# Splitting the weights of the backward pass: single steps through the end of the attention pass, none on GpSimd, a third in the next pass

## The chip, the cores and the metric

The kernel runs on one core of one Trainium2 chip. The metric is the device time of one execution in microseconds (us). A core has TensorE for matrix products (PE in the profile, its weight loads PEld), VectorE (DVE), ScalarE (ACT), GpSimd (POOL) and the DMA queues, of which SyncE (SP) issues most. Each engine takes its instructions in a fixed order; an instruction that waits holds everything behind it on its engine. About 0.2% is what a measurement of this kernel can tell from no change.

## The reference

One layer of a bidirectional encoder over 4096 rows of 1024 values, float32, in two groups of heads behind one normalised input projection.

```python
hn = rms_norm(x, norm_w)
proj = hn @ w_in                       # all groups' columns at once
qk_a = silu(conv5(qk_a))               # group A: centred depthwise conv over 5 rows
h = sigmoid(o_a) * (mlstm(q, k, v, i_f, f_f) + flip(mlstm(flip(q), flip(k), flip(v), i_b, f_b)))
y_a = head_rms_norm(h) * silu(z_a)     # 4 heads x 128, chunks of 128 rows
y_b = windowed_gqa(q_b, k_b, v_b, sink, rel_bias) * silu(z_b)   # |i-j| <= 128, 8 heads / 2 kv heads x 64
out = rms_norm(x + concat(y_a, y_b) @ w_out, final_norm_w)
```

The gate logits of group A go through `log_sigmoid`, running sums and running maxima along the rows before the two scans can use them.

## The kernel before

The kernel makes float32-like products from a cheaper format: each operand is split into a rounded part and the remainder, and three products (high x low, low x high, high x high) are added in one PSUM bank. A weight is split in two steps: ACT writes the rounded part scaled by the row's norm weight `nw`, DVE writes the remainder (`scalar_tensor_tensor`).

The work goes in passes. The **attention pass** (`pass1`) takes the rows in 16 blocks of 256 (`b`), with 32 chunks of 128 (`n`). It projects queries (`qproj`, tile `qp`, evicted by DVE at L538), keys (`kproj`, `kp`) and values and gates (`vproj`, `vp`, gates added by POOL at L509), and does the windowed attention of group B in **slots**: slot `sl` is one chunk and one of two kv heads. A slot is a list of up to ten pieces: scores of the slot after next (`att_a`, tile `sp`, evicted at L362 with row maxima; L369 makes the shift `st`), transposes of its probabilities (`att_t`, `tp`, split into `pt` by ACT L389 and DVE L390), and products with the values of the slot before (`att_o`, tile `op`, L401). `op` has one PSUM bank; ACT (L413) and DVE (L414) bring it into `ab`, which has one buffer too, and SP sends `ab` to DRAM (L416). The next slot's first `op` waits for L414.

TensorE's order is written by hand. `interleave(fill, pieces)` spreads the projections' matmuls (`fill`, with costs) evenly between the pieces: piece i comes when i/len(pieces) of the filler's cost is done. The other engines' orders are made from it by a scheduler, which follows the order of the program but lets ready work go ahead. `behind(c, ins)` holds an instruction back until `ins` stands.

The last three blocks run as one list, `pieces`, with **hooks** inserted at positions: the gate computations `gate1` to `gate3`, and `w2_load(j, c0)`, which loads and splits the weights that the next pass needs: values (j = 0), keys (j = 1) and queries (j = 2) of group A, each as 8 steps `k` of 128 rows x 512 columns. A step has a staging tile `w2s` of the tag `xf` (two buffers); every fourth step is scaled and subtracted on GpSimd (L554, L556) with a cast on ACT (L555), the others go through ACT (L558) and DVE (L559). The filler ends with the first value products of group A (`v2_units`, tile `v2p`).

The **backward pass** (`pass2`) goes through eight blocks of 512 rows from the last to the first: values (`v2p`, L829), keys (`qkproj` with m = 4 to 7) and queries (m = 0 to 3; tile `up`, L856; DVE does the convolution at L874 and L877), transposes of keys (`ktp`, tile `kt`, four buffers), weighting of the values (`weigh`: `wvr`, `wvh`, `wvl`) and state products (`kvp`, tile `kv`, L158 to L160; state `C`). `place(fill, pieces)` puts `ktp` and `kvp` at given shares of the filler. Block 7, the first that is done, uses the rows still on the chip; the loads `xb` of block 6 are issued during it.

## Time and profile before

| | before |
|---|---|
| median of 3 runs | 2211.6 us |
| lowest, highest | 2209.2, 2212.46 us |
| the profiled execution's own time | 2211.38 us |
| its span, first to last instruction | 2209.7 us |
| granted TensorE clock, mean | 0.994 |
| PE busy | 2163.6 us, 98% |
| DVE, ACT, POOL busy | 1409.6, 1086.3, 608.1 us |
| chain that ended last | PE 77%, DMA 8%, issue 5%, DVE 5%, ACT 2%, POOL 2% |

A line of groups names the source line, the engine, the operation, the tiles written and read, the shape and the count; then busy time and the mean of one in ns, and the idle time before them with what ended it. In the list by time the first numbers are start and length; the brackets hold the idle time before and its releaser. The attention pass lasts up to about 609 us; the weights in question are loaded and split from 444 to 599 us of the span.

### The profile page before, as it was taken

Reading aid. Unit: us, or ns where it says so; the run is one execution under the profiler, and the core shown is the slowest. Engines: PE = TensorE matmul, PEld = TensorE weight load, DVE = VectorE, ACT = ScalarE, POOL = GpSimd, SP = SyncE. Lnnn points to the kernel's source line nnn. Section 1 sums busy time; section 2 is a strip of 40 time slices with the busy share of each in tenths; the row PEclk is TensorE's granted clock in tenths of the full one; section 3 lists DMA queues with packets and bytes.
Section 4 is the critical chain, followed back from the end, with each engine's and each line's share of the span. In section 5 each row is a group of like instructions: output and inputs, shape, how many; then the busy total and the mean of one; then the engine's idle time right before and its main releaser. Section 6 shows DMA issues by size and latency. Waiting matters only on the chain.

```text
span 2209.7 us, 35186 instructions
## 1 busy us (share of the span) xinstructions
PE 2163.6 (98%) x12226; PEld 1878.6 (85%) x12226; DVE 1409.6 (64%) x3090; ACT 1086.3 (49%) x2711; POOL 608.1 (28%) x1059
## 2 busy tenths in 40 slices
PE   7999999999999999999999999999999999999998
PEld 6899999998797888888887888888888888888886
DVE  4677777777874575566568645455554443867776
ACT  5788888886743343344345444444443321433333
POOL 2565665662121211121112111112111111112222
PEclk9999999999999999999999999999999999999999
DMA  7663555432224442454166976877685899666765
GB/s 234 187 162 110 171 141 127 157 108 77 87 78 130 159 146 67 142 163 142 58 212 198 324 229 217 250 228 219 222 259 185 298 353 294 186 180 189 199 187 147
DMA packets 249126, 398.98 MB, mean 181 GB/s; under 512 B 21971, under 2 KB 128467, under 8 KB 248948
## 3 DMA queue, kind: packets, MB, share of 16 engines
q1 hardware_dynamic: 220628, 303.57, 45.3%
q0 software_dynamic: 28176, 92.96, 13.0%
q8 instruction: 96, 1.57, 0.3%
q14 instruction: 82, 0.67, 0.1%
q10 hardware_dynamic: 144, 0.20, 0.0%
HBM read 275.99 MB, written 120.67 MB: 180 GB/s over the span
## 4 chain that ended last, share of the span: by engine, by line
PE 77%; DMA 8%; issue 5%; DVE 5%; ACT 2%; POOL 2%; SPq 0%; POOLq 0%; DVEq 0%; ACTq 0%
PE up L856 15%; PE zp L1153 7%; PE qp L524 7%; PE op L1153 7%; PE v2p L829 7%; DMA xr<-x 5%; PE op L401 4%; PE tp L387 3%; PE sp L359 3%; PE zbp L158 3%; PE zbp L160 3%; PE zbp L159 3%; PE num L1106 3%; PE num L1105 2%; PE o L1320 2%
## 5 line engine op out<-in xcount | busy, mean ns | idle before, releaser
L856 PE MATMUL up<-xb,w 128*128 128x512 f32 x1344 | 338.4, 396 | 0.0
L1320 PE MATMUL o<-wo,yo 128*128 128x512 f32 (+1 forms) x1356 | 312.2, 392 | 0.0
L1320 PEld LDWEIGHTS o<-wo,yo 128*128 128x128 f32 x1356 | 253.2, 188 | 59.1
L856 PEld LDWEIGHTS up<-xb,w 128*128 128x128 f32 x1344 | 243.7, 188 | 47.2
L874 DVE SCALAR_TENSOR_TENSOR qk<-U,cw,qk 128x512 f32<-128x512 f32 x256 | 190.1, 755 | 94.2 <-ACT qk L872 89.4
L524 PE MATMUL qp<-xT,wqb 128*128 128x256 f32 x1536 | 246.3, 291 | 0.0
L524 PEld LDWEIGHTS qp<-xT,wqb 128*128 128x128 f32 x1536 | 218.0, 193 | 9.9 <-issue 1.7
L1153 PE MATMUL op<-w,xs 128*128 128x512 f32 x720 | 201.7, 407 | 0.0
L1153 PE MATMUL zp<-w,xs 128*128 128x512 f32 x720 | 187.9, 401 | 1.5 <-DVE z L1163 1.5
L829 PE MATMUL v2p<-w,xb 128*128 128x512 f32 x672 | 157.9, 395 | 1.9 <-DMA xb<-xT_d 1.9
L1153 PEld LDWEIGHTS zp<-w,xs 128*128 128x128 f32 x720 | 130.9, 189 | 28.4 <-DVE z L1163 2.0
L829 PEld LDWEIGHTS v2p<-w,xb 128*128 128x128 f32 x672 | 126.0, 188 | 32.5 <-DMA xb<-xT_d 3.2
L362 DVE CUSTOM_DVE_ANT_0 s<-sp,G 128x320 f32<-128x320 f32 (+1 forms) x256 | 122.8, 480 | 42.6 <-PE sp L359 39.4
L390 DVE TENSOR_TENSOR pt<-tp,pt 128x512 fp32r<-128x512 f32 x188 | 129.3, 688 | 26.6 <-ACT pt L389 25.1
L371 ACT ACTIVATE s<-s,st 128x320 f32<-128x320 f32 (+1 forms) x256 | 139.8, 549 | 12.0 <-DVE st L369 11.5
L1153 PEld LDWEIGHTS op<-w,xs 128*128 128x128 f32 x720 | 126.7, 189 | 20.9
L389 ACT CAST pt<-tp 128x512 fp32r<-128x512 f32 x188 | 110.0, 586 | 61.2 <-PE tp L387 58.4
L1120 ACT ACTIVATE hs<-num,r 128x128 f32<-128x128 f32 x128 | 47.1, 368 | 182.4 <-DVE r L1117 155.4
L401 PE MATMUL op<-pt,v 128*128 128x512 f32 x376 | 121.6, 405 | 11.7 <-DVE ab L414 11.7
L359 PE MATMUL sp<-kk,q 128*128 128x320 f32 (+2 forms) x512 | 118.9, 313 | 0.0
L387 PE MATMUL tp<-ident,s 128*128 128x128 f32 x752 | 113.9, 274 | 1.5 <-DVE pt L390 1.2
L1143 POOL DMA_DIRECT2D y_d<-ya x32 | 19.4, 607 | 325.4 <-ACT hs L1120 182.5
(273 smaller groups left out, 4530.1 us busy)
## 6 DMA issues: line engine op xcount, KB each, us to landing
xc<-xT_d SPq DMA_DIRECT2D x64, 512.0 KB, 8.0
xs<-xT_d SPq DMA_DIRECT2D x120, 256.0 KB, 6.5
xT_d<-xT POOLq DMA_DIRECT2D x104, 256.0 KB, 5.2
xb<-xT_d SPq DMA_DIRECT2D x48, 514.0 KB, 10.1
E<-m_d SPq DMA_DIRECT2D x64, 256.0 KB, 4.8
W<-w_d SPq DMA_DIRECT2D x64, 256.0 KB, 5.8
y<-y_d SPq DMA_DIRECT2D x32, 512.0 KB, 3.4
out<-xr POOLq DMA_DIRECT2D x31, 512.0 KB, 4.3
```

What stands on the lines that cost most here:

```text
L359: nc.tensor.matmul(sp[:, lo:hi], qt, kk[:, kv, z, col - 128 + lo:col - 128 + hi], start=(z == 0), stop=(z == 1))
L362: nc.vector.tensor_tensor_reduce(out=s[:, lo:hi], in0=sp[:, lo:hi], in1=bias[0][:, kv * 2 + m, lo - 64 * half:hi - 64 * half], op0=ALU.add ...
L371: nc.scalar.activation(ps[g][:, kept(g)], ps[g][:, kept(g)], AF.Exp, bias=ng[:, g:g + 1], accum_out=rs[:, g:g + 1])
L387: nc.tensor.transpose(tp[:, g * 128:(g + 1) * 128], ps[g][:, j * 128:(j + 1) * 128], c.ident)
L390: nc.vector.tensor_sub(pt[:, 1, :], tp, f32(pt[:, 0, :]))
L401: nc.tensor.matmul(op, vt, pt[:, z, :], start=(i == 0 and z == 0), stop=(i == len(js) - 1 and z == 1))
L524: nc.tensor.matmul(qp, wq[k // 2][:, k % 2, w, m * 128:m * 128 + 128], x[k], start=(k == 0 and j == 0), stop=(k == KT - 1 and j == 2))
L829: nc.tensor.matmul(vp, a, wv[k // 2][:, k % 2, m, :], start=(k == 0 and j == 0), stop=(k == KT - 1 and j == 2))
L856: nc.tensor.matmul(up[:, 0:hi - lo], w[k // 2][:, k % 2, a, cs], x, start=(k == 0 and j == 0), stop=(k == KT - 1 and j == 2))
L874: nc.vector.scalar_tensor_tensor(acc, U[:, t:t + 512], cw[:, cm, t:t + 1], acc, ALU.mult, ALU.add)
L1153: nc.tensor.matmul(P[nm], XS[n](a, k), w[:, m, :], start=(k == 0 and j == 0), stop=(k == KT - 1 and j == 2))
L1320: nc.tensor.matmul(p, a[:, z, k, :], w[k // 2][:, k % 2, m, lo:hi], start=k == 0 and z == 1, stop=k == 3 and z == 0 and m == 0)
```

## The change

`w2_load` is replaced by `w2_piece(j, k)`, one step of 128 rows, for values and keys alone. Values' steps 0 to 3 go into the slots of the last regular block (b = 12), steps 4 to 7 at positions 42 to 50 of the final list, keys' steps 0 to 7 at positions 68 to 96, four apart. All steps are split by ACT and DVE (`w2_split`); the load is held behind the last `at_d` transfer and the split behind the last small exponential of ACT. `gate1` is cut in three parts at positions 54, 58 and 62 instead of one at 80. The queries' weights (j = 2) are loaded at the start of the backward pass into the four `kt` buffers, two steps at once, and split behind the key projections m = 5 and m = 6 of block 7; the first `kvp` of that block comes at 44/96 of the filler instead of 34/96.

```diff
-        def w2_load(j, c0):
-            out = []
-            for k in range(KT):
...
-                st = wk.tile([128, 512], F32, tag="xf", bufs=2, name=f"w2s{j}{k}")
-                nc.sync.dma_start(st, A["w_in"][k * 128:k * 128 + 128, c0:c0 + 512])
-                s = c.nw[:, k:k + 1]
-                if k % 4 == 0:
-                    nc.gpsimd.tensor_tensor(out=st, in0=st, in1=s.broadcast_to([128, 512]), op=ALU.mult)
-                    nc.scalar.copy(w[:, k % 2, 0, :], st)
-                    nc.gpsimd.tensor_tensor(out=w[:, k % 2, 1, :], in0=st, in1=f32(w[:, k % 2, 0, :]), op=ALU.subtract)
-                    continue
-                nc.scalar.activation(w[:, k % 2, 0, :], st, AF.Copy, scale=s)
-                nc.vector.scalar_tensor_tensor(w[:, k % 2, 1, :], st, s, f32(w[:, k % 2, 0, :]),
-                                               ALU.mult, ALU.subtract)
+        def w2_piece(j, k):
...
+            st = wk.tile([128, 512], F32, tag="xf", bufs=2, name=f"w2s{j}{k}")
+            with behind(c, LAST["at"]):
+                nc.sync.dma_start(st, A["w_in"][k * 128:k * 128 + 128, 512 * j:512 * j + 512])
+            with behind(c, LAST["act"]):
+                w2_split(c, w, st, k)
...
+            if b == NB - 4:
+                for i in range(4):
+                    A2.insert(3 + 5 * i, lambda i=i: w2_piece(0, i))
...
-        hooks = [(40, lambda: w2_load(0, 0)), (80, lambda: gate1(c, wk)), (100, lambda: gate2(c, wk)),
-                 (104, lambda: w2_load(1, 512)), (113, lambda: gate3(c, wk)), (113, lambda: w2_load(2, 1024))]
+        hooks = [(p, lambda k=k: w2_piece(0, k)) for k, p in zip(range(4, 8), (42, 44, 48, 50))]
+        hooks += [(54 + 4 * i, lambda i=i: gate1(c, wk, i)) for i in range(3)]
+        hooks += [(68 + 4 * k, lambda k=k: w2_piece(1, k)) for k in range(8)]
+        hooks += [(100, lambda: gate2(c, wk)), (113, lambda: gate3(c, wk))]
...
+def w2_split(c, w, st, k):
+    s = c.nw[:, k:k + 1]
+    c.nc.scalar.activation(w[:, k % 2, 0, :], st, AF.Copy, scale=s)
+    c.nc.vector.scalar_tensor_tensor(w[:, k % 2, 1, :], st, s, f32(w[:, k % 2, 0, :]), ALU.mult, ALU.subtract)
...
-        wv, wk_, wq = c.w2
+        wv, wk_ = c.w2
+        wq = [wtile(c, [128, 2, 2, 512], f"w2_2{j}") for j in range(4)]
+
+        wqs = []
+        for j in range(4):
+            wqs.append(wk.tile([128, 2, 512], F32, tag="kt", bufs=4, name=f"w2s2{j}"))
+            nc.sync.dma_start(wqs[j], win_src(c, 2 * j, 2, 1024, 512))
+
+        def w2q(js):
+            with behind(c, c.ucopy):
+                for j in js:
+                    for i in range(2):
+                        w2_split(c, wq[j], wqs[j][:, i], 2 * j + i)
...
+                if b == 7 and m in (5, 6):
+                    w2q((0, 1) if m == 5 else (2, 3))
...
-            at += [((34 + 62 * (4 * (n3 - n) + hh) / 16) / 96, lambda n=n, hh=hh: kvp(n, hh))
+            k0 = 44 if b == 7 else 34
+            at += [((k0 + (96 - k0) * (4 * (n3 - n) + hh) / 16) / 96, lambda n=n, hh=hh: kvp(n, hh))
                    for n in range(n3, n3 - 4, -1) for hh in range(NH)]
```

Three places on DVE show what this does to the order. In the names, `w2_JK` is the weight j = J, of the pair of steps that begins with K, and `w2sJK` the staging tile of step K; the digits behind `pt`, `tp`, `sp`, `op` are the slot, behind `ab` and `vg` the chunk; the last number only counts.

DVE at the end of block 12, up to the eviction of slot 50 into `ab25`, before:

```order
L499 TENSOR_TENSOR vg28_6976<-vp28_6937,vg28_6976 128x144
L362 ISA s1_5_161,st53_6932<-sp53_3_7017,G_91 128x320
L362 ISA st53_6932 128x1
L559 SCALAR_TENSOR_TENSOR w2_00_7491<-w2s01_7497,nw_88,w2_00_7491 128x512
L369 SCALAR_TENSOR_TENSOR st53_6932<-st53_6932,nsink_228 128x4
L390 TENSOR_TENSOR pt51_1_6998<-tp51_1_6993,pt51_1_6998 128x512
L362 ISA s0_0_150,st54_7056<-sp54_0_7057,G_91 128x320
L362 ISA st54_7056 128x1
L414 TENSOR_TENSOR ab25_7007<-op50_6942,ab25_7007 64x2x4x64
```

and with the change:

```order
L499 TENSOR_TENSOR vg28_6990<-vp28_6946,vg28_6990 128x144
L636 SCALAR_TENSOR_TENSOR w2_02_6951<-w2s02_6952,nw_88,w2_02_6951 128x512
L636 SCALAR_TENSOR_TENSOR w2_02_6951<-w2s03_7000,nw_88,w2_02_6951 128x512
L362 ISA s1_5_161,st53_6941<-sp53_3_7037,G_91 128x320
L362 ISA st53_6941 128x1
L390 TENSOR_TENSOR pt51_1_7018<-tp51_1_7013,pt51_1_7018 128x512
L503 TENSOR_TENSOR v28_6993<-vg28_6990,v28_6993 128x2x64
L369 SCALAR_TENSOR_TENSOR st53_6941<-st53_6941,nsink_228 128x4
L362 ISA s0_0_150,st54_7074<-sp54_0_7075,G_91 128x320
L362 ISA st54_7074 128x1
L376 RECIPROCAL R_92<-st52_6827 128x4
L414 TENSOR_TENSOR ab25_7032<-op50_6958,ab25_7032 64x2x4x64
```

Two splits, of steps 2 and 3, stand where one of step 1 stood; steps 0 and 1 now stand as another pair ahead of `ab24`.

DVE ahead of the eviction of slot 56 into `ab28`, in the final list, before:

```order
L390 TENSOR_TENSOR pt57_0_7674<-tp57_0_7669,pt57_0_7674 128x512
L362 ISA s1_4_160,st59_7646<-sp59_2_7692,G_91 128x320
L538 SCALAR_TENSOR_TENSOR q15_1_7678<-qp15_1_7607,q15_1_7678 64x4x64 x2
L559 SCALAR_TENSOR_TENSOR w2_12_8177<-w2s12_8178,nw_88,w2_12_8177 128x512
L559 SCALAR_TENSOR_TENSOR w2_12_8177<-w2s13_8182,nw_88,w2_12_8177 128x512
L390 TENSOR_TENSOR pt57_1_7704<-tp57_1_7699,pt57_1_7704 128x512
L362 ISA s1_5_161,st59_7646<-sp59_3_7720,G_91 128x320
L414 TENSOR_TENSOR ab28_7713<-op56_7654,ab28_7713 64x2x4x64
```

and with the change:

```order
L636 SCALAR_TENSOR_TENSOR w2_06_7589<-w2s06_7590,nw_88,w2_06_7589 128x512
L636 SCALAR_TENSOR_TENSOR w2_06_7589<-w2s07_7631,nw_88,w2_06_7589 128x512
L390 TENSOR_TENSOR pt57_0_7665<-tp57_0_7660,pt57_0_7665 128x512
L362 ISA s1_4_160,st59_7638<-sp59_2_7697,G_91 128x320
L660 TENSOR_SCALAR g0_7678<-g0_7678 128x256
L538 SCALAR_TENSOR_TENSOR q15_1_7689<-qp15_1_7627,q15_1_7689 64x4x64 x2
L661 RECIPROCAL g0_7678<-g0_7678 128x256
L390 TENSOR_TENSOR pt57_1_7709<-tp57_1_7704,pt57_1_7709 128x512
L414 TENSOR_TENSOR ab28_7718<-op56_7647,ab28_7718 64x2x4x64
```

The two splits moved up by a few instructions, and the gate chain's first steps (`g0`, with the reciprocal) stand here, which came some three slots later before.

DVE at the start of the backward pass, block 7, after the fourth instruction of the first key convolution, before:

```order
L877 SCALAR_TENSOR_TENSOR qk7_4_8390<-th7_4_8396,qk7_4_8390 128x512
L874 SCALAR_TENSOR_TENSOR qk7_5_8455<-U7_5_8400,cw_7932,qk7_5_8455 128x512 x4
L877 SCALAR_TENSOR_TENSOR qk7_5_8455<-th7_5_8461,qk7_5_8455 128x512
L744 COPY cl_8132<-mp_8530 128x4
L745 TENSOR_SCALAR cl_8132<-cl_8132 128x2
```

and with the change:

```order
L900 SCALAR_TENSOR_TENSOR qk7_4_8360<-th7_4_8366,qk7_4_8360 128x512
L897 SCALAR_TENSOR_TENSOR qk7_5_8425<-U7_5_8370,cw_7672,qk7_5_8425 128x512
L636 SCALAR_TENSOR_TENSOR w2_20_8290<-w2s20_8294,nw_88,w2_20_8290 128x512
L897 SCALAR_TENSOR_TENSOR qk7_5_8425<-U7_5_8370,cw_7672,qk7_5_8425 128x512
L636 SCALAR_TENSOR_TENSOR w2_20_8290<-w2s20_8294,nw_88,w2_20_8290 128x512
L636 SCALAR_TENSOR_TENSOR w2_21_8291<-w2s21_8296,nw_88,w2_21_8291 128x512
L897 SCALAR_TENSOR_TENSOR qk7_5_8425<-U7_5_8370,cw_7672,qk7_5_8425 128x512
L636 SCALAR_TENSOR_TENSOR w2_21_8291<-w2s21_8296,nw_88,w2_21_8291 128x512
L897 SCALAR_TENSOR_TENSOR qk7_5_8425<-U7_5_8370,cw_7672,qk7_5_8425 128x512
```

Four of the eight splits of the queries' weights stand between the steps of one convolution; the other four stand between those of the next.

More of the change, by code (lines that the diff above doesn't have):

```diff
@@ L542, in qproj @@
             return [(lambda m=m, k=k, j=j: unit(m, k, j)) for m in range(4) for k in range(KT) for j in range(3)]
[L544 to L561 removed]
+        def w2_piece(j, k):
+            if k == 0:
+                c.w2.append([])
+            if k % 2 == 0:
+                c.w2[j].append(wtile(c, [128, 2, 2, 512], f"w2_{j}{k}"))
+            w = c.w2[j][k // 2]
+            st = wk.tile([128, 512], F32, tag="xf", bufs=2, name=f"w2s{j}{k}")
[3 more added lines that the diff above has]
+                w2_split(c, w, st, k)
         def v2_units(ns):
@@ L662, in gate1 @@
     nc.vector.tensor_scalar(e, f, 0.0, None, ALU.min)
-    nc.vector.scalar_tensor_tensor(c.GF.rearrange("p a h n -> p (a h n)"), p, -2.0, e, ALU.mult, ALU.add)
+    nc.vector.scalar_tensor_tensor(f, p, -2.0, e, ALU.mult, ALU.add)
     tri = c.tri = wk.tile([128, 2, 128], F32, tag="vg", bufs=2, name="tri")
```

45 lines of the change are left out of this document (24 added, 21 removed).

## The prediction

> **What bounds the kernel now.** The page first, for who is busy; then TensorE's own list of waits, for what holds it; then the granted clock by stretch; then the other engines' instructions in order of time around the longest wait.
>
> ```profile
> span 2209.7 us, 35186 instructions
> PE 2163.6 (98%) x12226; PEld 1878.6 (85%) x12226; DVE 1409.6 (64%) x3090; ACT 1086.3 (49%) x2711; POOL 608.1 (28%) x1059
> PE op L401 <- DVE ab L414: 11.7, 7, 3.5
> ```
>
> TensorE is busy 98% of the span, and its largest wait is `op`, the probabilities times values, on `ab`, the eviction of the one PSUM bank that `op` has. The list of TensorE's instructions with their idle time puts it (start, length, then in brackets the idle before and its releaser):
>
> ```profile
> 502.25 1.22 PE L401 MATMUL op<-pt,v 128*128 128x512 f32 x2 [3.51 <-DVE ab L414]
> 513.71 0.73 PE L401 MATMUL op<-pt,v 128*128 128x512 f32 x2 [0.65 <-DVE ab L414]
> 558.26 0.73 PE L401 MATMUL op<-pt,v 128*128 128x512 f32 x2 [1.59 <-DVE ab L414]
> 568.37 0.73 PE L401 MATMUL op<-pt,v 128*128 128x512 f32 x2 [1.76 <-DVE ab L414]
> 601.63 0.73 PE L401 MATMUL op<-pt,v 128*128 128x512 f32 x2 [1.07 <-DVE ab L414]
> 646.93 0.39 PE L159 MATMUL kv<-wvl,kt 128*128 128x258 f32 x1 [1.64 <-DVE wvl L920]
> 677.18 3.21 PE L829 MATMUL v2p<-w,xb 128*128 128x512 f32 x12 [1.47 <-DMA xb<-xT_d]
> 680.80 9.53 PE L829 MATMUL v2p<-w,xb 128*128 128x512 f32 x40 [0.41 <-DMA xb<-xT_d]
> ```
>
> So the change's own stretch, 440 to 680 us, holds 8.58 us of `op` waits over half a microsecond (five of them), 1.64 us for `wvl` and 1.88 us for `xb`. Idle time is not the whole loss. The clock falls behind two of these waits (windows: length, five engines' busy time with counts, clock, DMA share, GB/s):
>
> ```profile
> 502.00:504.00 2.00, 1.75 (x6) 1.55 (x7) 1.21 (x4) 1.73 (x6) 0.71 (x5) 0.50 0.28 96
> 504.00:506.00 2.00, 2.00 (x11) 2.00 (x11) 1.10 (x4) 0.00 (x0) 0.60 (x1) 0.50 0.37 131
> 506.00:508.00 2.00, 2.00 (x11) 1.86 (x10) 1.05 (x4) 0.58 (x1) 0.00 (x0) 0.61 0.43 104
> 568.00:570.00 2.00, 1.63 (x5) 1.35 (x6) 1.97 (x5) 2.00 (x9) 0.00 (x0) 0.75 0.70 223
> 570.00:572.00 2.00, 2.00 (x9) 1.70 (x9) 0.79 (x4) 0.06 (x1) 1.20 (x2) 0.50 0.51 147
> 572.00:574.00 2.00, 2.00 (x10) 1.68 (x10) 0.69 (x1) 1.72 (x3) 0.54 (x1) 0.90 0.10 35
> ```
>
> Busy time times the missing clock is lost: 1.75 x 0.50 + 2.00 x 0.50 + 2.00 x 0.39 = 2.65 us behind the first, 1.63 x 0.25 + 2.00 x 0.50 + 2.00 x 0.10 = 1.61 us behind the second, 4.26 us together. All that the change can win on TensorE is then about 8.6 + 4.3 + 1.6 + 1.9 = 16.4 us, 0.7% of the span.
>
> **What makes `ab` late.** DVE and GpSimd in order of time before the 3.51 us:
>
> ```profile
> 497.18 1.84 DVE L559 SCALAR_TENSOR_TENSOR w<-w2s,nw,w 128x512 fp32r<-128x512 f32 x1
> 498.95 1.65 DVE L369 SCALAR_TENSOR_TENSOR st<-st,nsink 128x4 f32<-128x4 f32 x1
> 501.53 0.67 DVE L414 TENSOR_TENSOR ab<-op,ab 64x512 f32<-64x512 f32 x1
> 513.69 0.16 DVE L369 SCALAR_TENSOR_TENSOR st<-st,nsink 128x4 f32<-128x4 f32 x1
> 497.17 1.30 POOL L556 TENSOR_TENSOR w<-w2s,w 128x512 fp32r<-128x512 f32 x1
> 498.42 1.11 POOL L509 TENSOR_TENSOR G<-vg,gb 128x4 f32<-128x4 f32 x4
> 499.49 1.08 POOL L265 TENSOR_TENSOR xT<-xraw,xT 128x512 fp32r<-128x512 f32 x1
> L559 DVE SCALAR_TENSOR_TENSOR w<-w2s,nw,w x18: 737/751/1844, 497.2 to 599.5; 128x512 fp32r<-128x512 f32 x18
> ```
>
> One split took 1.84 us where the median of 18 is 0.75, and the small `st` behind it 1.65 us where another took 0.16: 1.09 + 1.49 = 2.58 us of stretch, while GpSimd ran L556, L509 and L265 without a gap. Both stretched instructions read two operands from SBUF; the `ab` behind them reads one from PSUM and took 0.67, as `ab` does elsewhere. The Trainium skill, GPSIMD Engine Reference, section Key points, says that GpSimd shares its SBUF interfaces with VectorE and contends with instructions that have two SBUF inputs; the rows agree, and the rule speaks against this change too, for L509 and L265 stay while the number of splits beside them grows.
>
> **The change part by part.** The matmuls are the same. Removed from GpSimd are six multiplications and six subtractions; DVE and ACT take them over:
>
> ```profile
> L554 POOL TENSOR_TENSOR w2s<-w2s,nw x6: 1030/1040/1042, 446.9 to 581.9; 128x512 f32<-128x512 f32 x6
> L556 POOL TENSOR_TENSOR w<-w2s,w x6: 1278/1297/1516, 497.2 to 593.4; 128x512 fp32r<-128x512 f32 x6
> L558 ACT ACTIVATE w<-w2s,nw x18: 706/723/731, 496.4 to 598.5; 128x512 fp32r<-128x512 f32 x18
> ```
>
> GpSimd loses 6 x (1.04 + 1.30) = 14.0 us. DVE goes from 18 to 24 splits: +6 x 0.75 = 4.5 us. But by place: 4 now fall before 500 us (one before), 12 between 500 and 600 us (17 before), 8 into the next pass (none). Per place:
>
> First pair (k = 0 and 1, ahead of `ab24`). Nothing stood there. Two casts on ACT, 2 x 0.72 us, and two splits on DVE, 2 x 0.75 us, now stand ahead of the `pt` and `ab` of their slot, and behind that `ab` waits the first `op` of the next slot. The nearest row for a split ahead of an `ab` is the 0.65 us at 513.71. I take +0.5; bounds 0 (DVE's idle time takes the 1.5 us) and 1.5 (none of it does).
>
> Second pair (k = 2 and 3, ahead of `ab25`), the 3.51 us place. Before: one split, 2.58 us of stretch. Now a second split, +0.75, and L556 gone from GpSimd, while L509 and L265 remain and a cast of keys (L466) moves in between. Without any stretch the wait would be 3.51 - 2.58 + 0.75 = 1.7 us; with as much as before 4.3 us. I take 3.2, nearer the upper end, since what remains on GpSimd, 1.11 + 1.08 us, again begins when the `vg` ahead of the pair is done. So -0.3.
>
> Clock behind it: a wait of 3.2 us is nearest to the 3.51 that lost 2.65, so 0 change; bounds -2.65 and 0. By the Trainium skill, TensorE: Matmul & The Clock Gate, Part 1, the clock is halved only after an idle window of about 3.4 us; the row at 568.37, half clock behind 1.76 us, says that less is enough here, so I do not lean on it.
>
> The waits of 0.65, 1.59 and 1.76. Two splits stood directly ahead of the second of these `ab`, one ahead of each other. Now a split comes with every fourth piece, and as each piece gets the same share of the filler (132 pieces instead of 121, 17 of them hooks instead of 6), a slot that holds splits gets a tenth more TensorE time to hide them and one without gets a tenth less. I take all three waits as gone: -4.0 us; bounds -4.0 and 0. Each load follows an `at_d` on SP's queue, so none stands ahead of the transfer that `ab`'s single buffer needs; 20 issues instead of 24 cost nothing there. What comes instead is the gate chain, moved forward to where queries are still projected:
>
> ```profile
> L538 DVE SCALAR_TENSOR_TENSOR q<-qp,q 64x256 fp32r<-64x256 f32 x30 | 12.7, 422 | 1.7 <-ACT q L534 1.2
> L655 DVE RECIPROCAL g<-g 128x256 f32<-128x256 f32 x1 | 1.7, 1747 | 0.0
> 576.28 0.68 DVE L414 TENSOR_TENSOR ab<-op,ab 64x512 f32<-64x512 f32 x1 [0.18 <-ACT ab L413]
> 585.63 0.69 DVE L414 TENSOR_TENSOR ab<-op,ab 64x512 f32<-64x512 f32 x1
> ```
>
> Before, the reciprocal and its neighbours with two splits filled 9.35 us from one `ab` to the next without a wait. Now two stretches follow each other that share the chain and hold four evictions of queries each, 4 x 0.42 = 1.7 us, the first with two splits, the second without. I take 0.8 us; bounds 0 (as before) and 2.0 (both 1 us over). A clock drop behind it, 1.6 us, I weigh at a fifth: 0.3. The 1.07 at 601.63 stands where the attention runs out and three evictions follow closely; without the two splits ahead of it I take 1.0, since it also hangs on ACT.
>
> Next pass. Eight casts and splits, 8 x 0.75 = 6.0 us of DVE, go in between the convolutions. DVE is idle there (rows of DVE):
>
> ```profile
> 609.52 17.34 PE L856 MATMUL up<-xT,w 128*128 128x258 f32 x144
> 622.43 3.18 DVE L874 SCALAR_TENSOR_TENSOR qk<-U,cw,qk 128x512 f32<-128x512 f32 x4 [1.16 <-ACT qk L872]
> 635.77 1.54 DVE L874 SCALAR_TENSOR_TENSOR qk<-U,cw,qk 128x512 f32<-128x512 f32 x2 [2.12 <-ACT qk L872]
> ```
>
> A product of 48 matmuls takes 17.34 / 3 = 5.8 us, so the fifth, the first to need these weights, begins behind 609.5 + 4 x 5.8 = 632.7 us, and its last weights are wanted 2 us later. From 622.43 DVE has 3.18 us of convolution and 6.0 us of splits to do, up to 631.6, and 3 us are left for the gate's small steps: 0 (bounds 0 and +1, a few more steps of 0.75 in front). The state products `kv` begin 10/96 of a filler of 192 matmuls of 0.12 us, so 2.4 us, later: the 1.64 us for `wvl` goes (bounds -1.64 and 0, if DVE is that much later too). TensorE then reaches `xb` 1.6 us sooner, while those loads wait for buffers that the same `kv` give free, 0.6 us sooner at best: +1.0 (bounds 0 and 1.6).
>
> Sum against the profiled execution, 2211.38 us: +0.5 - 0.3 - 4.0 + 0.8 + 0.3 - 1.61 (the clock at 568) - 0.07 - 1.64 + 1.0 = **-5.0 us, 2206.4 us**. That execution is 0.2 us below the median shown.
>
> **The rivals.**
>
> R1, the clock stays up: the second pair's wait comes out near its lower end, 1.7 us, and stays without a drop, as the 1.59 at 558.26 did. 2206.4 - 1.5 - 2.65 = 2202.2. For it: L556 is gone. Against: 568.37 dropped with 1.76. With the 3.4 us of the Trainium skill (TensorE: Matmul & The Clock Gate, Part 1) this would be the result.
>
> R2, the pairs take the gain back: the steps are single in the code, yet on DVE they stand in twos where the staging pair arrives together (the rows of the order), so the change does not do what it says. First pair 1.5, second 4.3, gate chain 2.0 with its drop: 2206.4 + 1.0 + 1.1 + 1.2 + 1.3 = 2211.0. For it: the rows. Against: the later pairs have the longer slots around them.
>
> R3, the other side, late staging in the next pass. Four loads of 512 KB are issued behind the last `at_d`:
>
> ```profile
> 601.60 9.19 SPq L416 DMA_DIRECT2D at_d<-ab x2
> at_d<-ab SPq DMA_DIRECT2D x32, 256.0 KB, 2.8
> wqbs<-w_in SPq DMA_DIRECT2D x4, 512.0 KB, 8.2
> w_0s<-w_in SPq DMA_DIRECT2D x4, 512.0 KB, 14.8
> ```
>
> 610.8 + 2.8 + 8.2 = 621.8 us is just in time for the first split (622.43 and one step of convolution, 623.1); with 14.8 it is 628.4 and 0.72 for the cast, so DVE stands 6.0 us in its own order with convolutions, key transposes and `wvl` behind it. TensorE would lose these 6.0 us, not win the 1.64, and drop its clock, 2.65: 2206.4 + 6.0 + 1.64 + 2.65 = 2216.7. It decides from a landing some 10 us after the issue. For it: the sibling `w_0s`. Against: DMA is at 0.18 of its share there (600 to 620 us) while `w_0s` loads collide with other traffic.
>
> ```profile
> 600.00:620.00 20.00, 18.93 (x131) 17.02 (x130) 9.85 (x17) 6.16 (x13) 2.34 (x13) 1.00 0.18 67
> ```
>
> **How the numbers follow.** Forecast 0.48, spread 2203.8 to 2208.8; R1 0.18; R2 0.18; R3 0.13; 0.03 for nothing of this kind. About 0.2%, 4.4 us, is what a measurement of this kernel tells from no change: below 2207.2 is faster, above 2216.0 slower. Faster: 0.62 of the forecast, 0.30, and R1, 0.18: 0.48. Slower: R3 and a fifth of R2, 0.16. The rest, 0.36, is same. The range reaches below R1 by the 2.2 us that the first pair, the gate chain and the 601.63 place can still give, and above R2 by half of the way to R3: 2199.5 to 2214.
>
> **What would show it.** Right: `op` waits of some 3 us near 499 us with half clock behind it, nothing over 1 us between 505 and 560, no `kv` wait on `wvl`, L636 never above 1.2 us after 505 us. Wrong: an `op` wait over 1.5 us behind the reciprocal (the gate chain was underpriced); `w` on ACT in the next pass waiting for its DMA (R3); a first-pair wait over 1.5 us; a clock of 1.00 throughout (R1).

## The result and the profile after

The changed kernel takes 2215.11 us, median of 20 runs (2212.28 to 2221.51), against 2212.57 us for the kernel before on the same chip (median of 20, 2209.2 to 2217.44). The ratio is 1.0014, 95% interval 1.0008 to 1.0021: slower by some 3 us, where 5.0 us less was forecast, and just outside the range. The profiled execution of the changed kernel is one of its shortest, 2212.42 us with a span of 2210.7 us.

The page and TensorE's own waits after, answering to those shown of before:

```profile
span 2210.7 us, 35163 instructions
PE 2164.5 (98%) x12226; PEld 1877.1 (85%) x12226; DVE 1407.3 (64%) x3096; ACT 1086.4 (49%) x2711; POOL 593.1 (27%) x1047
PE op L401 <- DVE ab L414: 10.6, 7, 3.0
PE op L1179 <- ACT o L1187: 4.2, 1, 4.2
PE ktp L927 <- DVE qk L900: 1.1, 1, 1.1
```

GpSimd lost 15 us of work, the wait for `ab` only 1.1 us, and there is a wait that no list of before has: L1179 for ScalarE's `o`, 4.2 us at once. L1179 is a product of the third pass, some 550 us behind the last place in the trace that the change touches (the first `kvp` of block 7, near 645 us). The list of TensorE's instructions by time, with the places that the prediction spoke of and the new one:

```profile
491.90 0.72 PE L401 MATMUL op<-pt,v 128*128 128x512 f32 x2 [1.28 <-DVE ab L414]
502.39 1.22 PE L401 MATMUL op<-pt,v 128*128 128x512 f32 x2 [2.95 <-DVE ab L414]
529.11 0.53 PE L359 MATMUL sp<-kk,q 128*128 128x320 f32 x2 [0.85 <-DVE q L538]
537.76 0.74 PE L401 MATMUL op<-pt,v 128*128 128x512 f32 x2 [0.95 <-DVE ab L414]
557.11 0.74 PE L401 MATMUL op<-pt,v 128*128 128x512 f32 x2 [0.62 <-DVE ab L414]
567.40 0.73 PE L401 MATMUL op<-pt,v 128*128 128x512 f32 x2 [1.53 <-DVE ab L414]
598.93 0.74 PE L401 MATMUL op<-pt,v 128*128 128x512 f32 x2 [0.71 <-DVE ab L414]
669.97 4.72 PE L852 MATMUL v2p<-w,xb 128*128 128x512 f32 x18 [0.57 <-DMA xb<-xT_d]
1204.21 7.38 PE L1179 MATMUL op<-w,xb 128*128 128x512 f32 x24 [4.22 <-ACT o L1187]
```

The wait of `kv` for `wvl` is gone. What has become of the rest is best seen when the same matmul is looked up in both traces. Both have 12226 of them; between those of the same number, in us, with TensorE's idle time in brackets:

```
                                        before          changed
  480 to  604 us, matmul 3450 to 4200   123.9 (9.17)    121.7 (9.18)   end of the attention pass
  604 to  663 us, 4200 to 4650           59.3 (2.33)     56.9 (0.39)   start of the backward pass
  663 to 1204 us, 4650 to 7200          540.7 (3.70)    540.8 (2.89)   rest of it
 1204 to 1249 us, 7200 to 7450           44.8 (1.29)     49.2 (4.22)   start of the third pass
 1249 to 2201 us, 7450 to 12225         952.5 (1.53)    953.1 (0.77)   all that follows
```

In its own stretch the changed execution gained 2.2 + 2.4 = 4.6 us, close to the 5.0 forecast; how much of this belongs to the change is taken up with the second experiment. Then 4.4 us were lost at one place that the prediction never looked at. (The changed kernel's execution was also 1.2 us ahead at 480 us, before anything was changed, and lost 1.7 us behind the last matmul, 1.1 of it where a row norm on ScalarE waits for a load of `x`, 4.29 us against 3.19. Neither belongs to the change: in the second experiment, which has the code of before at both places, they are 1.4 us ahead and 1.8 us lost.)

What stands at that place: the rows of ScalarE and SyncE in order of time, changed, then before.

```profile
1198.93 0.57 SPq L902 DMA_DIRECT2D q_d<-qk  x1
1203.52 0.32 SPq L1087 DMA_DIRECT2D lq<-q_d  x1
1203.56 0.60 ACT L1187 ACTIVATE o<-op 128x512 f32<-128x512 f32 x1 [5.93 <-DMA q_d<-qk]
1204.05 0.59 ACT L1187 ACTIVATE z<-zp 128x512 f32<-128x512 f32 x1
```

```profile
1203.12 0.58 ACT L1161 ACTIVATE o<-op 128x512 f32<-128x512 f32 x1
1204.53 0.57 SPq L879 DMA_DIRECT2D q_d<-qk  x1
1205.66 0.60 ACT L1161 ACTIVATE z<-zp 128x512 f32<-128x512 f32 x1 [1.96 <-PE zp L1153]
```

`o` is the tanh of a product; it has nothing to do with `q_d`, the store of the last convolved queries of the backward pass. Before, it ran 1.4 us ahead of that store's issue. Now it waits for the store to land. The waits are put there by the program: in the two built programs ScalarE has different ones at this instruction (DMAHW6 and DMAHW7 are the semaphores of the stores of `qk0_2` and `qk0_3`):

```
before   L1161 ACTIVATE o0<-op0 128x512 [waits PE]
changed  L1187 ACTIVATE o0<-op0 128x512 [waits DMAHW6, DMAHW7, DVE, PE]
```

The reason is memory. A pool gives its tags room in the order in which they are first asked for, and the pools of the second and third pass start at the same byte. The change stages the third matrix in the tag `kt` and asks for it first of all. The bytes of each partition, from the built programs:

```
                             before               changed
second pass  qk (4 buffers)  188320 to 196512     204704 to 212896
             kt (4 buffers)  198560 to 214944     179744 to 196128
third pass   o0              208544 to 210592     208544 to 210592
```

Before, `o0` lay on `kt`, whose last readers are matmuls long done. Now it lies on two `qk` buffers, and those are being stored when `o0` is written. The diff shows the tag; it does not show the address. TensorE has two banks for these products, so it stops at the third, 4.22 us, and half clock follows (windows, clock third from the end):

```profile
1204.00:1206.00 2.00, 1.79 (x6) 1.48 (x7) 0.69 (x1) 2.00 (x8) 0.00 (x0) 0.76 0.69 215
1206.00:1208.00 2.00, 2.00 (x7) 1.54 (x6) 1.23 (x1) 0.96 (x4) 0.00 (x0) 0.50 0.93 282
1208.00:1210.00 2.00, 2.00 (x9) 1.65 (x8) 0.00 (x0) 0.00 (x0) 0.00 (x0) 0.88 1.01 365
```

### The profile page after: what moved, and what is told of

Same layout as the page of the kernel before. It is cut to its first block, busy times and chain, and to the rows that moved or that the text cites. A ratio compares the mean times of both kernels' runs of the same rounds, so it can differ in the third digit from the quotient of the medians.

```text
span 2210.7 us, 35163 instructions
## 1 busy us (share of the span) xinstructions
PE 2164.5 (98%) x12226; PEld 1877.1 (85%) x12226; DVE 1407.3 (64%) x3096; ACT 1086.4 (49%) x2711; POOL 593.1 (27%) x1047
## 4 chain that ended last, share of the span: by engine, by line
PE 78%; DMA 9%; issue 5%; DVE 4%; ACT 2%; POOL 2%; SPq 0%; POOLq 0%; ACTq 0%; DVEq 0%
PE up L879 15%; PE op L1179 8%; PE zp L1179 7%; PE qp L524 7%; PE v2p L852 7%; DMA xr<-x 5%; PE op L401 4%; PE tp L387 3%; PE sp L359 3%; PE zbp L158 3%; PE zbp L160 3%; PE zbp L159 3%; PE num L1132 3%; PE num L1131 2%; PE kp L460 2%
## 5 line engine op out<-in xcount | busy, mean ns | idle before, releaser
L1179 PE MATMUL op<-w,xs 128*128 128x512 f32 x720 | 202.5, 408 | 0.0
L1179 PE MATMUL zp<-w,xs 128*128 128x512 f32 x720 | 188.1, 402 | 0.8 <-DVE z L1189 0.8
L1179 PEld LDWEIGHTS zp<-w,xs 128*128 128x128 f32 x720 | 130.8, 188 | 27.9 <-DVE z L1189 1.2
L1179 PEld LDWEIGHTS op<-w,xs 128*128 128x128 f32 x720 | 126.7, 189 | 21.5
```

Of the source, the lines that this page charges most:

```text
L1179: nc.tensor.matmul(P[nm], XS[n](a, k), w[:, m, :], start=(k == 0 and j == 0), stop=(k == KT - 1 and j == 2))
```

## The experiments

The expectations number the kernels in the order in which they were built: 1, the changed one with the old addresses; 2, the one before with the new addresses; 3, all three matrices in the attention pass; 4, the first with its first four splits late; 5, the one before without GpSimd's splits; 6, the one before with the third matrix in the next pass; 7, the fourth with the first matrix spread; 8, the fourth with the gate chain later; 9, the fifth and sixth parts together; 10, all spread; 11, the first with the gate chain later. Twelve to fifteen are the first, eleventh, fourth and eighth again.

Ratios are against the kernel before, run on the same chip beside them, with 95% intervals. The first four kernels ran on one chip, where the kernel before took 2212.28 us, the others on a second, where it took 2215.9 to 2216.9 us; microseconds are compared only on one chip.

### Places alone: the old ones under the change, the new ones under the kernel before

First, the changed kernel with the tags claimed in the old order; no instruction is added.

```diff
+        for tag, shape, n in (("C", [128, NH, 129], 2), ("U", [128, 516], 2), ("hl", [128, 8, 4], 2),
+                              ("qk", [128, 512], 4), ("th", [128, 512], 1)):
+            for i in range(n):
+                wk.tile(shape, F32, tag=tag, bufs=n, name=f"claim_{tag}{i}")
         wqs = []
```

> The changed kernel, with one thing added: at the start of the next pass its pool is asked once for the tiles C, U, hl, qk and th, before the four staging tiles kt, so that every tile of that pass lies at the address it had before the change. No instruction is added. Theory A (places): the changed kernel first asks for kt, which moves the q tiles by 16384 bytes, and so in the third pass the tile o lies on the q tile whose store is still under way; ScalarE's o then waited 5.93 us for that store, TensorE 4.22 us, with 3.4 us of half clock behind it, and the lead over the kernel before fell from 5.6 to 1.1 us there. By A that wait is gone here, no TensorE wait over 1 us stands between 1190 and 1230 us, and the median comes to 2215.1 - 4.5 = 2210.6 us (0.999 of before). Rival B (the lead is real only in the profiled execution, and the changed kernel is slower all along, by lower clock in other executions): the median stays at 2214 to 2216 us, whatever stands at the start of the third pass. Rival C (the store is only late, and the next reader of q waits in its place): the wait moves to the load of q or the score product, and the median stays above 2213.

Second, the kernel before with `kt` claimed first.

```diff
+        for i in range(4):
+            wk.tile([128, 2, 4, 128], F32R, tag="kt", bufs=4, name=f"claim_kt{i}")
         C0 = wk.tile([128, NH, 129], F32, tag="C", bufs=2, name="C_init")
```

> The kernel before, with one thing added: at the start of the next pass its pool is asked first for the four kt tiles, so that every tile of that pass lies where it lies in the changed kernel. No instruction is added or moved. Theory A (places): the wait of ScalarE's first o for the store of q appears here too, TensorE waits 4 to 5 us at the third block of products of the third pass (near 1205 us) with 3.4 us of half clock behind it, and the median rises by 4.5 to 6 us to 2217 to 2218.5 us (1.002). Rivals B and C (the places do not matter to the time): 2212 to 2213.5 us, no TensorE wait over 1.5 us there.

Measured: the first 2210.76 us, 0.9995 (0.9986 to 1.0003); the second 2215.73 us, 1.0018 (1.0009 to 1.0026). ScalarE's `o` in the first, then in the second:

```profile
1199.64 0.58 ACT L1191 ACTIVATE o<-op 128x512 f32<-128x512 f32 x1
```

```profile
1207.43 0.60 ACT L1163 ACTIVATE o<-op 128x512 f32<-128x512 f32 x1 [5.88 <-DMA q_d<-qk]
```

and TensorE in the second:

```profile
1208.08 7.28 PE L1155 MATMUL op<-w,xb 128*128 128x512 f32 x24 [4.12 <-ACT o L1163]
```

The same stretch (matmul 7200 to 7450) lasts 44.7 us in the first and 49.0 in the second. Theory A holds both ways: the address costs 4 us (1.0014 against 0.9995, and 1.0018 against 1), and nothing waits in its place but 1.27 us of the score product for its load, as 1.29 before. C falls, and B with its median of 2214 to 2216 us. The rise of the second was put at 4.5 to 6 us and is 4.0 (2.0 to 5.8). But the first kernel only equals the kernel before: of the 4.6 us gained in the changed stretch, most is not in the median.

The second kernel shows why, for up to 1204 us it runs the instructions of the kernel before. Its end of the attention pass (matmul 3450 to 4200) took 121.8 us with 9.28 us idle, where the same code took 123.9 in the profile of before: it had 3.4 us of half clock there, and that profile 10.2. So the 2.2 us of that row are no more than two executions of one code differ by, and the changed places in the attention pass have no gain to show. The 2.4 us at the start of the backward pass are real: 59.3, 59.4 and 59.4 us in the three profiles (before, second and fifth kernel) with the third matrix split as before, 56.8 to 57.0 in all thirteen with it in the next pass. What remains had to be taken apart.

### The first four splits

The first kernel with steps 0 to 3 of the first matrix taken out of block 12 and put where the kernel before began.

```diff
-            if b == NB - 4:
-                for i in range(4):
-                    A2.insert(3 + 5 * i, lambda i=i: w2_piece(0, i))
...
-        hooks = [(p, lambda k=k: w2_piece(0, k)) for k, p in zip(range(4, 8), (42, 44, 48, 50))]
+        hooks = [(p, lambda k=k: w2_piece(0, k)) for k, p in zip(range(8), (40, 40, 40, 40, 42, 44, 48, 50))]
```

> The first kernel of this study (the changed one with the old addresses), and the first four splits moved back from the block that ends near 505 us to where the kernel before began them. Asks what the first two pairs of splits on VectorE cost where the change put them: the profile shows TensorE 1.28 us late at 491.9 and 2.95 us at 502.4 us, against none and 3.51 us before, with half clock for 3.4 us against 6.8 us. By the sum of the prediction (first pair +0.5, second pair -0.3, and the three later waits of 4.0 us removed by what was moved forward): 2 to 4 us slower than the first kernel, 2213 to 2214.5 us, with TensorE waits for VectorE of over 1.5 us between 545 and 570 us. By the rival that the moved pairs cost as much as they spare: within 1 us of the first kernel.

Measured: 2204.81 us, 0.9973 (0.9963 to 0.9983), 6 us faster than the first kernel. The expectation had the sign wrong. Neither the wait at 492 nor that at 502 us is there any more, and not even the 3.51 us of the kernel before; of VectorE's waits over 1 us one is left, later:

```profile
555.31 1.22 PE L401 MATMUL op<-pt,v 128*128 128x512 f32 x2 [2.87 <-DVE ab L414]
```

Matmul 3450 to 4200 lasts 117.2 us (idle 5.69) against 123.9 (10.03) in the first kernel. Why the pair cost so much where the change put it shows in the changed kernel's rows around 498 us:

```profile
492.31 0.99 SPq L552 DMA_DIRECT2D w2s<-w_in  x2
497.34 1.39 ACT L635 ACTIVATE w<-w2s,nw 128x512 fp32r<-128x512 f32 x2 [1.96 <-DMA w2s<-w_in]
498.10 1.88 DVE L636 SCALAR_TENSOR_TENSOR w<-w2s,nw,w 128x512 fp32r<-128x512 f32 x2 [1.22 <-ACT w L635]
```

The two loads are issued at 492.31 and land 5 us later. ScalarE, at the casts in its fixed order, stands 1.96 us; VectorE stands 1.22 us behind it, and then the pair takes 1.88 us. Together 3.1 us on VectorE ahead of `ab`, about the wait of 2.95. GpSimd's part in it is about 0.5 us: the first split of the pair took 1.22 us, beside GpSimd's cast of keys (L466), where the other 23 took 0.72 to 0.75. That moving the four removes these waits is shown; that it is the late load which makes them is read from these rows, and no kernel with an earlier load was run.

### One part of the change alone, on the kernel before

No GpSimd, nothing else:

```diff
-                if k % 4 == 0:
-                    nc.gpsimd.tensor_tensor(out=st, in0=st, in1=s.broadcast_to([128, 512]), op=ALU.mult)
-                    nc.scalar.copy(w[:, k % 2, 0, :], st)
-                    nc.gpsimd.tensor_tensor(out=w[:, k % 2, 1, :], in0=st, in1=f32(w[:, k % 2, 0, :]), op=ALU.subtract)
-                    continue
```

> The kernel before with one part of the change alone: the steps k=0 and k=4 of each of the three matrices are split by ScalarE and VectorE like the others, none on GpSimd; places, gate chain and the next pass as before. The profile before shows, beside GpSimd's steps near 497 us, a split of 1.84 us where the others take 0.75, and a sink step of 1.65 us where others take 0.16, and then TensorE's wait of 3.51 us with 6.8 us of half clock behind it. Theory E (GpSimd's work beside VectorE's stretches those two): VectorE's queue there falls from 3.5 us to 0.75 + 0.75 + 0.16 = 1.7 us, the wait near 502 us falls to 1.0 to 1.8 us with no half clock or 3.4 us of it, and the median falls by 3 to 5 us to 2207 to 2209 us. Theory F (at that place any split holds VectorE for as long as the attention can bear; two splits of 0.75 to 0.94 us cost as much as one stretched): the wait stays at 2.8 us or more, and the median within 1.2 us of the kernel before, 2211 to 2213.5.

The third matrix in the next pass, at the old addresses, nothing else (`claim` as in the first kernel, `w2q` and `k0` as in the change):

```diff
-                 (104, lambda: w2_load(1, 512)), (113, lambda: gate3(c, wk)), (113, lambda: w2_load(2, 1024))]
+                 (104, lambda: w2_load(1, 512)), (113, lambda: gate3(c, wk))]
```

> The kernel before with one part of the change alone: the third matrix is loaded at the start of the next pass and split there beside that pass's first products, which start their weighted products later, as in the changed kernel, and the tiles of that pass are kept at their old addresses. The first two matrices, GpSimd's steps in them and the gate chain stay as before. By the sum of the prediction: the product's wait of 1.64 us for its low weights is gone, and waits on the loads of xb are 1.0 us longer or, as the profile of the changed kernel shows them, 1.0 us shorter: -0.6 to -2.6 us, 2209.7 to 2211.7 us. By the third kernel of this study, in which the same third at the end of the attention pass cost 10 us against the first kernel: up to 8 us faster, 2204 to 2206 us, but the kernel before shows no such loss at that place (its U is copied without delay), which speaks for the smaller figure.

Both together:

> The kernel before with the two parts that gained alone, and nothing else: no split on GpSimd (0.9968 of before alone) and the third matrix in the next pass with its tiles at the old addresses (0.9982 alone). The splits of the first two matrices still stand in one piece each where they were, and the gate chain too. If the two parts are independent, the ratio is about 0.995 (0.994 to 0.996), as good as the best so far (0.9950), and the single steps and the places of the first four add nothing. If the single steps are worth something of their own, this kernel stays at 0.9965 or above.

Measured: without GpSimd 0.9968 (0.9956 to 0.9981), by the ratio 7 us where 3 to 5 were expected; the third in the next pass 0.9982 (0.9973 to 0.9991), 4 us, more than the 0.6 to 2.6 of the prediction's terms; both 0.9962 (0.9951 to 0.9974). Each part alone is worth more than the whole change at the old addresses (0.9995 and, run again, 0.9999), though the intervals of the third in the next pass and of these just touch. The rows of the first of the three near 502 us:

```profile
499.95 0.75 DVE L554 SCALAR_TENSOR_TENSOR w<-w2s,nw,w 128x512 fp32r<-128x512 f32 x1
501.03 0.74 DVE L554 SCALAR_TENSOR_TENSOR w<-w2s,nw,w 128x512 fp32r<-128x512 f32 x1
502.29 0.60 DVE L369 SCALAR_TENSOR_TENSOR st<-st,nsink 128x4 f32<-128x4 f32 x1
503.95 0.74 PE L401 MATMUL op<-pt,v 128*128 128x512 f32 x2 [1.86 <-DVE ab L414]
```

Two splits of 0.75 and a `st` of 0.60 us, 2.1 us in all, where one split of 1.84 and a `st` of 1.65 stood. The wait fell from 3.51 to 1.86 us and no half clock followed in that execution (with both parts together the same wait of 1.86 us had 3.4 us of it). Theory E holds, with 1.86 just above its 1.8: with the GpSimd split gone, the split at its place ran in 0.75 us. The Trainium skill, GPSIMD Engine Reference, section Key points, has GpSimd contend with VectorE's instructions of two SBUF inputs. The rows agree, but not for every GpSimd instruction: the split at 501.03 ran beside L509 (128x4) and took 0.74 us. In the kernel with the third alone the wait for `wvl` is gone and matmul 4200 to 4650 takes 56.8 us, as in the changed kernel. Both together fall between the 0.995 of two independent parts and the 0.9965 at which single steps would have had a worth of their own, and decide neither.

### All three matrices in the attention pass

The changed kernel with the third matrix's eight steps as pieces at position 113, `k0 = 34`, and no staging in the next pass:

```diff
+        hooks += [(113, lambda k=k: w2_piece(2, k)) for k in range(8)]
...
-        wv, wk_ = c.w2
+        wv, wk_, wq = c.w2
```

> The changed kernel with its last third undone: the third matrix (wq) is split in single steps at the end of the attention pass, where the kernel before split it, and the weighted products of the next pass's first block start where they did before. GpSimd still splits nothing, the first two matrices and the gate chain stand as changed. The staging tiles of the next pass are gone, so its tiles lie at the old addresses. Theory A (places, and the lead as the profile shows it): no wait at the start of the third pass; of the lead of 4.6 us that the change had won by 660 us, the 2.6 us between 640 and 680 us (the product waiting 1.64 us for its low weights, and 1.0 us of waits on loads) are not won, so 2210.6 + 2.6 = 2213.2 us (1.0003). Rival D (the third in the next pass is worth nothing, and the gain comes from the first pass alone): 2210.6 us or less. Rival B: 2214 to 2216 us.

Measured: 2221.42 us, 1.0039 (1.0025 to 1.0053), 10.7 us slower than the first kernel, against 2.6 expected. Two of TensorE's waits, and the last cast on ScalarE:

```profile
533.14 0.87 PE L359 MATMUL sp<-kk,q 128*128 128x320 f32 x2 [2.74 <-DVE q L538]
627.61 4.63 PE L868 MATMUL up<-xT,w 128*128 128x256 f32 x24 [2.61 <-ACT U L872]
626.57 0.72 ACT L636 ACTIVATE w<-w2s,nw 128x512 fp32r<-128x512 f32 x1 [2.98 <-DMA w2s<-w_in]
```

With two staging buffers the last casts wait for their loads one after the other, and ScalarE, standing 2.98 us at the last of them, holds the copy of `U` behind it and with it TensorE, 2.61 us: what R3 feared of the next pass happens here, in the order that the change left. The wait at 533 us is not explained by that; the eight further pieces also thin out the filler between all pieces, which may be its cause and was not tried by itself. So this kernel mixes two things, and the one that moves the third matrix alone is the better evidence on it.

### The order of what is left

From the kernel with the late four: its eight splits spread three apart; the gate chain later, with six of the second matrix's splits moved ahead of it; and all of it four apart.

```diff
-hooks = [(p, ...) for k, p in zip(range(8), (40, 40, 40, 40, 42, 44, 48, 50))]
+hooks = [(p, ...) for k, p in zip(range(8), range(29, 53, 3))]
```

> The fourth kernel of this study with the eight splits of the first matrix three attention pieces apart (29 to 50) in place of four at 40 and four at 42 to 50. That kernel has one wait of VectorE's left that is over 1 us: 2.87 us at 555.3 us, ahead of which VectorE did two splits of 0.74, gate steps of 0.42 and 0.29 and the gate chain's reciprocal of 1.74 us. If the splits' crowding makes that wait, it falls under 1 us and the median comes to 2201 to 2202.5 us; if the reciprocal does, the wait stays over 2 us and the median within 1.2 us of 2204.8.

```diff
-        hooks += [(54 + 4 * i, lambda i=i: gate1(c, wk, i)) for i in range(3)]
-        hooks += [(68 + 4 * k, lambda k=k: w2_piece(1, k)) for k in range(8)]
+        hooks += [(56 + 4 * k, lambda k=k: w2_piece(1, k)) for k in range(6)]
+        hooks += [(79 + 4 * i, lambda i=i: gate1(c, wk, i)) for i in range(3)]
+        hooks += [(90 + 4 * k, lambda k=k: w2_piece(1, 6 + k)) for k in range(2)]
```

> The fourth kernel of this study with the three pieces of the gate chain later (at 79, 83 and 87 of the attention pieces in place of 54, 58 and 62), near where the kernel before had them, and the second matrix's first six splits ahead of them. If the gate chain's reciprocal of 1.74 us makes the wait of 2.87 us at 555.3 us, that wait is gone, and a wait of 1 to 2 us stands where the chain now is (the kernel before had 1.59 and 1.76 us there): median 2203 to 2204.5. If the chain was well placed before, the same wait of about 2.9 us moves with it and the median is 2204 to 2206.5.

> The eighth kernel of this study with the splits of the first matrix four attention pieces apart (38 to 66), then the gate chain (70, 74, 78), then the second matrix four pieces apart (82 to 110): no two splits at neighbouring places by the table. If crowding of splits on VectorE makes what is left of the waits (0.88, 0.66, 0.73, 0.80 and 0.56 us in the eighth), the idle time of TensorE in the last attention blocks falls from 3.6 to under 2.5 us and the ratio to 0.994 to 0.9945; if the order on VectorE makes them whatever the table says, 0.995 or above.

Measured: 0.9961 (0.9948 to 0.9973), 0.9950 (0.9938 to 0.9963) and 0.9955 (0.9943 to 0.9966). The first broke the 2.87 us into four waits of 0.88 to 1.32 us and left their sum (idle in matmul 3450 to 4200: 5.74 us, 5.69 without the spread): neither of its two expectations came true. With the chain later nothing over 0.88 us is left in that stretch (idle 3.62, stretch 113.5 us), and no wait stands at the chain's new place, less than the 1 to 2 us expected. Spreading everything cut the idle time to 2.96 us, short of the 2.5 set, and did not move the time further: the stretch itself still lasts 113.6 us. Behind it TensorE waits for the loads of `xb`, as in every kernel here, 2.3 us in this one and between 0.8 and 3.6 in the others, so the place where the lead ends is not shown:

```profile
668.59 11.67 PE L854 MATMUL v2p<-w,xb 128*128 128x512 f32 x49 [2.04 <-DMA xb<-xT_d]
```

### The gate chain, on one chip

The first kernel with the three pieces of the gate chain's first step together at position 80, between the second matrix's splits:

```diff
-        hooks += [(54 + 4 * i, lambda i=i: gate1(c, wk, i)) for i in range(3)]
-        hooks += [(68 + 4 * k, lambda k=k: w2_piece(1, k)) for k in range(8)]
+        hooks += [(68 + 4 * k, lambda k=k: w2_piece(1, k)) for k in range(4)]
+        hooks += [(80, lambda i=i: gate1(c, wk, i)) for i in range(3)]
+        hooks += [(68 + 4 * k, lambda k=k: w2_piece(1, k)) for k in range(4, 8)]
```

> The first kernel of this study (the changed one with the old addresses, 0.9995 of before) with the gate chain's first step in one piece between the second matrix's splits, near where the kernel before had it, in place of three pieces further forward. The prediction priced the move forward at +0.8 us and +0.3 us of clock, so by it this kernel is 1.1 us faster than the first, 0.999; the profile of the changed kernel shows waits of 0.62 and 1.53 us (0.87 and 1.55 in the first kernel of this study) at the chain's new place, so up to 2.4 us faster, 0.9984. If the old place is as crowded (the kernel before had waits of 1.59 and 1.76 us there with 3.4 us of half clock), it is the same or slower: 0.9995 to 1.0005.

Measured 0.9978 (0.9969 to 0.9987), more than either side expected, but on another chip than the first kernel. So four kernels were run together, early or late first splits with the chain forward or near its old place (the first, eleventh, fourth and eighth kernels again):

> The first kernel of this study again (the changed one with the old addresses), on one chip with the three after it: first four splits early, gate chain forward. By ratio it was 0.9995 of before on another day's chip, by microseconds 2210.8.

> The eleventh again: first four splits early, gate chain near its old place. Theory G (the forward move of the gate chain costs what its waits and the half clock behind them say, 118.4 against 123.9 us for the same products in the profiled executions): 0.15 to 0.25 per cent under the one before it, 3 to 5.5 us. Theory H (the difference of ratios was the chips'): within 0.07 per cent, 1.5 us. The prediction's own terms: 1.1 us.

> The fourth again: first four splits late, gate chain forward. If the early four cost what the fourth kernel showed (0.9973 against 0.9995), it is 0.2 to 0.25 per cent under the first of these four.

> The eighth again: both late. Theory G: 0.15 to 0.25 per cent under the one before it and 0.2 to 0.28 under the second of these four. Theory H: within 0.07 per cent of the one before it.

```
                       chain forward               chain near its old place
first four early       0.9999 (0.9987 to 1.0011)   0.9979 (0.9970 to 0.9988)
first four late        0.9973 (0.9961 to 0.9985)   0.9952 (0.9938 to 0.9966)
```

Theory G holds twice: moving the chain forward costs 0.20 and 0.21%, 4.1 us between the medians (2215.33 and 2211.23; 2209.83 and 2205.68). The early four cost 0.26 and 0.27%, 5.5 us. The two add. The chain's two moves are not quite the same: in the first pair its three pieces go together to position 80 and nothing else moves, in the second they go to 79, 83 and 87 and six splits of the second matrix move ahead of them. By the half widths of the intervals each difference is uncertain by some 3 to 4 us (an estimate), so 4.1 rests on the two agreeing. With the chain back, the waits of 0.79 and 1.54 us that the first of the four has at 562 and 572 us are gone and, unlike in the kernel before, no half clock falls there; TensorE's list of the second of the four has between 515 and 660 us, of waits over half a microsecond, only

```profile
534.61 0.53 PE L359 MATMUL sp<-kk,q 128*128 128x320 f32 x2 [0.85 <-DVE q L538]
543.26 0.74 PE L401 MATMUL op<-pt,v 128*128 128x512 f32 x2 [0.94 <-DVE ab L414]
602.75 0.73 PE L401 MATMUL op<-pt,v 128*128 128x512 f32 x2 [0.70 <-DVE ab L414]
```

The last of the four, first splits late, chain at its old place, old addresses, is the best version found: 2205.68 us against 2215.92, 0.48% less than the kernel before, and it was 0.9950 in its first run.

## Why the prediction was wrong

The steps in the order of the sum, predicted against the profiled execution of the changed kernel:

- **First pair**, +0.5 (0 to 1.5): 1.28 us at 491.90. Mis-sized within its bounds. Its own two splits took 0.75 us each; behind them a `st` that now stands ahead of `ab` took 1.45 us beside GpSimd's L265.
- **Second pair**, -0.3 by a wait of 3.2 us: 2.95, right. What was priced wrongly was the cause: the wait was put down to GpSimd's L509 and L265 going on; by the rows it is mostly a load that lands 5 us after its issue, and two casts in order behind it. The prediction looked for late staging loads only in the next pass (R3), where ScalarE's casts then waited for none.
- **Clock behind it**, 0 (-2.65 to 0): half clock for 3.4 us instead of 6.8 in the profiled execution, 6.8 again in the first experiment, none in the eleventh kernel. It does not follow from the length of the wait.
- **Waits of 0.65, 1.59 and 1.76 gone, -4.0, and the gate chain, +0.8 and +0.3.** This failed. The idle time in these 750 matmuls is 9.17 us before and 9.18 after: the waits went elsewhere. The four runs on one chip say which term: with the chain at its old place the waits are short (0.85, 0.94 and 0.70 left), if not gone, and the chain's move forward costs 4.1 us instead of 1.1. The sign that was named, an `op` wait over 1.5 us behind the reciprocal, is there in part: the first `op` wait behind the reciprocal (553.98) is the 0.62 us at 557.11, and the 1.53 at 567.40 stands behind the chain's third part.
- **Clock loss behind 568, -1.61**: gone, right.
- **Place at 601.63, -0.07**: 1.07 to 0.71, -0.36.
- **Next pass.** The eight splits cost nothing and the 1.64 us for `wvl` is gone, both right. The waits for `xb` were put 1.0 us longer; they were 1.0 us shorter in the profiled execution, 0.3 shorter in the first experiment, but 1.4 longer (0.82 and 2.42, with half clock) when the same program ran again among the last four. Right in kind, and different each time.

The sum of these for the stretch, -5.0, was met by -4.6 in the one profiled execution, in good part by luck of the clock: the end of the attention pass took 121.7, 123.9 and 121.9 us in three profiles with the change, and 123.9 and 121.8 in two without. In the median of the kernel at the old addresses little is left of it (0.9995 and 0.9999). The four signs named for a right forecast (waits of some 3 us near 499 with half clock, nothing over 1 us between 505 and 560, no wait on `wvl`, L636 under 1.2 us) are all there in the changed kernel, whose time went the other way: none of them looked beyond 680 us.

The step that cost most, 4.2 us, is not in the sum, which put it at nothing without a reason. "Four loads of 512 KB are issued behind the last `at_d`" was the whole treatment of the staging tiles: when they land was asked, not what their tag does to the pool. The sum ended at 680 us. None of the three rivals has this mechanism. R1, a wait of 1.7 us with the clock up, and R3, late staging in the next pass, are excluded by these rows of the changed kernel (a window with the clock third from the end, and casts that wait for no load):

```profile
502.00:504.00 2.00, 1.61 (x5) 1.42 (x6) 1.14 (x3) 1.77 (x7) 0.78 (x5) 0.50 0.37 131
619.00 2.55 ACT L635 ACTIVATE w<-w2s,nw 128x512 fp32r<-128x512 f32 x4
624.73 2.55 ACT L635 ACTIVATE w<-w2s,nw 128x512 fp32r<-128x512 f32 x4
```

R2 (the pairs and the chain take the gain back) is nearest to what remains once the address is set right, at the first four and at the chain. With the chain at 4.1 instead of 1.1 (+3.0) and 4.2 us for the address (1.0014 less 0.9995, of 2212.6), the forecast of 2206.4 would have been 2213.6 us: 2.2 us over the 2211.38 it was reckoned against, where the medians differ by 2.5. That it comes so near is in part luck: GpSimd's splits, whose removal alone is worth 7 us, and the early four, which cost 5.5 us, stand in the sum as two pairs at +0.5 and -0.3, and what both lack nearly cancels. (The range's lower end, 2199.5, lies 2.7 us below R1 and not the 2.2 of the text; nothing hangs on it.)

What stays open is how the rest divides. The waits on `xb` and the half clock change from one execution of a program to the next by as much as the terms that are left, so a single profile cannot share out the last 2 us.

## What to carry to other kernels

A change that makes a pool give a tag room in another order moves every tile behind it, and the next pool's tiles with it: compare the addresses, and the waits of each instruction in the built programs, over the whole program and not only where the lines changed. Price a part against what remains when the other parts are done: the early splits looked free beside an old wait of 3.5 us that the removal of GpSimd's step would have shortened anyway. A split brought forward brings its load with it, and in a fixed order a late load stops both engines.

## What the runs showed of the hardware

- A tile of the third pass waited for a store out of two buffers that its bytes touch: 5.93 and 5.88 us on ScalarE, 4.22 and 4.12 on TensorE, from its neighbours' address alone.
- The half clock behind a given wait is not a fixed price. Behind the wait of 2.94 to 2.96 us it lasted 6.8 us in one profile and 3.4 in four, and was absent in a sixth (the eleventh kernel). Behind 3.51 us it lasted 6.8 us in the kernel before and 3.4 when that code ran again in the second experiment; behind 1.76 us 3.4 us in the kernel before, and none behind 1.75 us in the second experiment. The Trainium skill, TensorE: Matmul & The Clock Gate, Part 1, puts the drop at an idle window of about 3.4 us. The drop behind 1.76 us of idle time does not agree. The Trainium skill, TensorE: Matmul & The Clock Gate, Part 1, also says that this window runs freely. That would fit the changing lengths; no run here tests it.
- With GpSimd's split beside it removed, VectorE's split fell from 1.84 to 0.75 us and the small `st` from 1.65 to 0.60. The same holds over whole traces: in the kernel before, the 46 `st` that had no GpSimd instruction running beside them took 0.14 to 0.17 us, the other 18 up to 1.65, with a median of 0.89.
